# Conformer convolution stage: VectorE's taps kept out of the norms, the residual's bias and the rounding moved, two taps fewer for GpSimd

## The chip, the cores and the metric

One core of one Trainium2 chip runs the whole program. The metric is the device time of one execution in microseconds (us), as the median of three runs. TensorE (PE in the rows) multiplies, VectorE (DVE), ScalarE (ACT) and GpSimd (POOL) do the elementwise work, and SyncE's queue (SP) issues the DMAs.

## What is computed

Two layers of a diffusion trunk over 1024 latent tokens of width 1024, with 256 context tokens. Layer 0 mixes with differential attention and Fourier groups, layer 1 with a Conformer convolution; each is followed by a SwiGLU feed-forward. The change touches layer 1's mixer and the beginning of its feed-forward:

```python
def conformer_conv(h, pw1_w, pw1_b, dw_w, dw_b, ln_g, ln_b, pw2_w, pw2_b):
    a, g = jnp.split(h @ pw1_w + pw1_b, 2, axis=-1)
    u = a * jax.nn.sigmoid(g)
    u = depthwise_conv(u, dw_w) + dw_b          # 31 taps along the tokens, per channel
    u = jax.nn.silu(layernorm(u, ln_g, ln_b))
    return u @ pw2_w + pw2_b

x = x + mod_l[2] * conformer_conv(modulate(rmsnorm(x, mix_norm_g), mod_l[0], mod_l[1]), ...)
x = x + mod_l[5] * swiglu(modulate(rmsnorm(x, ffn_norm_g), mod_l[3], mod_l[4]), w1, w3, w2)
```

## The kernel before

Activations lie transposed: a tile is 128 channels by 512 tokens, so a tensor is 8 channel tiles (j = 0 to 7) in two halves of the tokens (h = 0, 1). Every product is made exact enough by splitting both operands into a rounded part and a rest (`hh`, `hl` for activations, `wh`, `wl` for weights, `uh`, `ul` for the feed-forward's hidden tiles): three matmuls of 512 columns for one (L95 to L97). The rounded part is a copy that rounds, the rest a subtraction. TensorE's order is written by hand from the end of layer 0 on. On the other engines a scheduler places what is not marked with `keep`; what is marked stays in the order in which it was written.

The convolution stage runs in this order on TensorE.

- **Cells**: the products of pw1, one per channel tile and half. ScalarE takes the sigmoid (`sig`, L1269), VectorE the gated product `u` (L1271), and then the 31 taps of the tile are shared out. GpSimd takes `NPA` = 11 taps of half 0 and `NPB` = 12 of half 1: ScalarE scales a window (`pr`, L1191), GpSimd adds it to `acc` (L1192). VectorE takes the others as chains in PSUM (`cs`, L1158, L1161), then joins GpSimd's sum (L1167) and writes the tile (`acc`, L1170). A planner with rough costs (`work`, `took`, `clock`) decides, each time that TensorE gets a block of work, how many taps VectorE and GpSimd get behind it.
- **Layer norm of half 0**: `ln_first` subtracts the mean on VectorE (L1296), squares on ScalarE (L1298) and sums on TensorE (L1299). `neg_rstd` makes the reciprocal root, `ln_apply` multiplies (L1328), takes Silu (L1329), rounds to `hh` (L1331) and subtracts to `hl` (L1332). Two cells stand between sum and use.
- **pw2 of half 0** (`pw2_half`): eight products; the first two together, channel tile by channel tile, as `hh` and `hl` arrive. The residual `xt` has gate times bias added (L1351), each product is flushed into it (L914), squares are summed on VectorE (`nacc`), and one matmul (L180) sums them over the channels for the next norm. One cell, then `norm_apply` (L1377 to L1388).
- **Units**: the feed-forward of half 0 begins while taps of half 1 still run. A unit f makes one hidden tile (48 matmuls, then `gate`: L940 to L943), a unit j adds two output tiles (24 matmuls, flushed by L914). They come as four f, four j, and so on. `while left(1): unit(...)` goes on until no tap of half 1 is left; then come mean, `ln_center`, `ln_var`, `ln_apply` and pw2 of half 1, with `POSB` units between them, and the last units.

The lists `LNH` and `LNL` say, channel tile by channel tile, whether VectorE makes `hh` and `hl` in `ln_apply`, or ScalarE and GpSimd.

## Time and profile before

| | |
|---|---|
| time, median of 3 runs (lowest to highest) | 2589.54 us (2587.44 to 2596.87) |
| the profiled execution: time, span | 2593.21 us, 2591.4 us |
| TensorE busy, share of the span | 2494.8 us, 96% |
| VectorE, ScalarE, GpSimd | 1428.6 us (55%), 1039.0 us (40%), 1025.1 us (40%) |
| granted TensorE clock, mean | 0.984 |

The span is the profiled time from the first to the last instruction; 1.8 us of the execution lie around it. Matmuls are pipelined, so that TensorE's busy time does not say that it runs at its peak; the count of matmuls in a stretch, set against their spacing, tells more. The clock is given as a share of 2.4 GHz; its two levels are 2.4 and 1.2 GHz.

### The profile page before, as it was taken

How to read it: one execution, taken by the hardware profiler on the slowest of the kernel's cores; microseconds unless marked ns; L12 is line 12 of the kernel's file. 1: busy time of each engine (PE TensorE's matmuls, PEld its weight loads, DVE VectorE, ACT ScalarE, POOL GpSimd, SP SyncE). 2: the span in 40 equal slices, each digit the busy share in tenths (PEclk: the TensorE clock that was granted, in tenths of full speed). 3: DMA queues.
4: the chain of work that ended last, by engine and by line, in shares of the span. 5: the costliest groups of instructions: out<-in, count | busy, mean ns of one | idle time of the engine just before them, and what ended most of it. 6: DMA issues, size and time to landing. Idle time of an engine off the chain costs nothing.

```text
span 2591.4 us, 30933 instructions
## 1 busy us (share of the span) xinstructions
PE 2494.8 (96%) x11818; PEld 2036.1 (79%) x11818; DVE 1428.6 (55%) x2028; ACT 1039.0 (40%) x1808; POOL 1025.1 (40%) x682
## 2 busy tenths in 40 slices
PE   8999979999999999999999999888998999999998
PEld 4788968778788888888788779666776788888887
DVE  4777359999564327262733569877946522222225
ACT  6321158988452121212121477565545422221113
POOL 2534032333443223232322358376982344431223
PEclk9999999999999999999999999989999999999999
DMA  9556643331522325242432355412333333321113
GB/s 342 190 181 223 185 140 81 83 90 31 165 66 90 114 78 175 82 146 81 149 96 71 115 169 181 139 58 81 98 90 106 94 94 97 98 81 49 46 47 120
DMA packets 350989, 299.35 MB, mean 116 GB/s; under 512 B 12341, under 2 KB 318458, under 8 KB 350842
## 3 DMA queue, kind: packets, MB, share of 16 engines
q1 hardware_dynamic: 349658, 293.16, 37.0%
q0 software_dynamic: 1184, 4.23, 0.5%
q8 instruction: 93, 1.52, 0.2%
q14 instruction: 54, 0.44, 0.1%
HBM read 259.07 MB, written 38.27 MB: 115 GB/s over the span
## 4 chain that ended last, share of the span: by engine, by line
PE 71%; DVE 7%; ACT 3%; POOL 2%; DMA 2%; issue 1%; DVEq 0%; SPq 0%; ACTq 0%; POOLq 0%
PE ps L97 20%; PE ps L95 20%; PE ps L96 20%; PE o L768 3%; PE s L740 2%; PE pst L751 2%; DVE p L886 1%; POOL acc L1192 1%; DVE cs L1161 1%; DVE acc L159 1%; PE sx L740 1%; POOL p L874 1%; DMA aw<-in_ada_w_dram 1%; ACT wh L85 1%; PE ps L809 0%
## 5 line engine op out<-in xcount | busy, mean ns | idle before, releaser
L86 POOL TENSOR_TENSOR wl<-wr,wh 128x1024 fp32r<-128x1024 f32 (+1 forms) x225 | 528.2, 2348 | 983.1 <-ACT wh L85 910.4
L95 PE MATMUL ps<-hh,wh 128*128 128x512 f32 (+2 forms) x2200 | 858.7, 390 | 15.6 <-ACT hh L1331 8.9
L97 PE MATMUL ps<-hl,wh 128*128 128x512 f32 (+2 forms) x2200 | 851.6, 387 | 9.3 <-POOL hl L1332 2.8
L96 PE MATMUL ps<-hh,wl 128*128 128x512 f32 (+2 forms) x2200 | 848.0, 386 | 3.2 <-DMA wl<-pd 2.0
L95 PEld LDWEIGHTS ps<-hh,wh 128*128 128x128 f32 x2200 | 416.5, 189 | 106.5 <-ACT hh L1331 10.9
L97 PEld LDWEIGHTS ps<-hl,wh 128*128 128x128 f32 x2200 | 416.6, 189 | 103.5 <-POOL hl L1332 5.4
L85 ACT CAST wh<-wr 128x1024 fp32r<-128x1024 f32 (+1 forms) x238 | 243.2, 1023 | 627.1 <-PE ps L97 467.6
L96 PEld LDWEIGHTS ps<-hh,wl 128*128 128x128 f32 x2200 | 417.3, 190 | 92.5 <-issue 3.1
L941 DVE TENSOR_TENSOR us<-us,ps 128x512 f32<-128x512 f32 x88 | 60.5, 687 | 596.5 <-PE ps L97 589.6
L95 PE MATMUL ps<-uh,wh 128*128 128x512 f32 (+1 forms) x728 | 281.8, 388 | 3.8 <-ACT uh L942 2.1
L97 PE MATMUL ps<-ul,wh 128*128 128x512 f32 (+1 forms) x728 | 279.8, 385 | 3.9 <-DVE ul L943 3.9
L96 PE MATMUL ps<-uh,wl 128*128 128x512 f32 (+1 forms) x728 | 278.1, 383 | 0.0
L1192 POOL TENSOR_TENSOR acc<-acc,pr 128x512 f32<-128x512 f32 x168 | 226.1, 1349 | 27.9 <-ACT pr L1191 19.7
L963 DVE SCALAR_TENSOR_TENSOR xt<-ps,mod,xt 128x512 f32<-128x512 f32 (+1 forms) x176 | 125.6, 722 | 131.4 <-PE ps L97 131.2
L159 DVE SCALAR_TENSOR_TENSOR acc<-aw,sc,acc 128x256 f32<-128x256 f32 x280 | 186.0, 664 | 20.0 <-DMA aw<-in_ada_w_dram 12.7
L1161 DVE SCALAR_TENSOR_TENSOR cs<-u,dwc,cs 128x512 f32<-128x512 f32 x280 | 194.8, 748 | 2.0 <-POOL u L1414 0.3
L943 DVE TENSOR_TENSOR ul<-us,uh 128x512 fp32r<-128x512 f32 x88 | 152.5, 1732 | 62.3 <-ACT uh L942 62.3
L97 PEld LDWEIGHTS ps<-ul,wh 128*128 128x128 f32 x728 | 137.1, 188 | 33.4 <-DVE ul L943 5.2
L95 PEld LDWEIGHTS ps<-uh,wh 128*128 128x128 f32 x728 | 137.1, 188 | 32.2 <-ACT uh L942 2.9
L96 PEld LDWEIGHTS ps<-uh,wl 128*128 128x128 f32 x728 | 137.2, 189 | 28.1 <-issue 0.7
L940 ACT ACTIVATE us<-ps 128x512 f32<-128x512 f32 x88 | 52.6, 598 | 252.9 <-PE ps L97 252.8
L874 POOL TENSOR_SCALAR p<-p,r 128x1280 f32<-128x1280 f32 x48 | 63.9, 1332 | 172.1 <-DVE r L873 132.2
(292 smaller groups left out, 3080.4 us busy)
## 6 DMA issues: line engine op xcount, KB each, us to landing
wr<-in_w_dram SPq DMA_DIRECT2D x162, 512.0 KB, 3.8
aw<-in_ada_w_dram SPq DMA_DIRECT2D x96, 512.0 KB, 4.2
wr<-in_pw_dram SPq DMA_DIRECT2D x64, 512.0 KB, 4.3
wl<-pd SPq DMA_DIRECT2D x32, 512.0 KB, 3.6
q<-qd SPq DMA_DIRECT2D x96, 128.0 KB, 2.9
wr<-in_w_dram SPq DMA_DIRECT2D x28, 384.0 KB, 3.2
wr<-in_w_in_dram SPq DMA_DIRECT2D x20, 512.0 KB, 4.3
wr<-in_w_out_dram SPq DMA_DIRECT2D x16, 512.0 KB, 4.2
```

The costliest lines, as they stand in the source:

```text
L85: S.copy(hi, src)
L86: (lo_eng or G).tensor_tensor(lo, src, hi.bitcast(F32), op=ALU.subtract)
L95: PE.matmul(ps, wh, xh, start=first, stop=False)
L96: PE.matmul(ps, wl, xh, start=False, stop=False)
L97: PE.matmul(ps, wh, xl, start=False, stop=last)
L159: V.scalar_tensor_tensor(a, aw[:, k, :], s1, a, op0=ALU.mult, op1=ALU.add)
L740: keep(PE.matmul(o, q[qt // 4][v][:, c, (qt % 4) * P:(qt % 4 + 1) * P], kk[:, c, k0:k0 + n], start=(v == 0), stop=(v == 1)))
L874: keep(G.tensor_scalar(y["p"][0], y["p"][0], r[:, 0:1], 1.0, op0=ALU.mult, op1=ALU.mult))
L943: V.tensor_tensor(ul, s, uh.bitcast(F32), op=ALU.subtract)
L963: V.scalar_tensor_tensor(XT[j][h][:, c], ps, mcol(self.l, 5, j), XT[j][h][:, c], op0=ALU.mult, op1=ALU.add)
L1161: keep(V.scalar_tensor_tensor(c["ps"], win(j, h, i), tap(i, j), c["ps"], op0=ALU.mult, op1=ALU.add))
L1192: keep(G.tensor_tensor(csum(j, h), csum(j, h), pr, op=ALU.add))
```

## The change

It has five parts. A list `quiet` stops the planner from handing taps to VectorE: from the end of half 0's taps until its pw2 begins, and again from pw2's seventh product until `norm_apply` is done. The gated bias `gb` is computed early, and the eight bias additions to the residual of half 0, not marked with `keep` and so free to go as early as `gb` exists, stand among the cells. ScalarE makes all eight `hh` of a layer norm, VectorE the `hl` of even tiles, GpSimd of odd ones, and ScalarE's steps keep their written order. GpSimd takes 10 taps of a half 1 tile and VectorE 21. The last square of a residual is no longer added on VectorE: TensorE sums `nacc` and that square in two matmuls. In units j the two outputs alternate by hidden tile. `POSB` becomes (0, 1, 2).

```diff
-NPA, NPB = 11, 12
+NPA, NPB = 11, 10
...
-LNH = (0, 1)
-LNL = (1, 1, 0, 1, 0, 1, 0, 1)
+LNL = (1, 0, 1, 0, 1, 0, 1, 0)
 NEG, NEF = 3, 3
-POSB = (0, 2, 1)
+POSB = (0, 1, 2)
...
-            d = chain() if clock["dve"] < t - TDVE / 2 else None
+            d = chain() if clock["dve"] < t - TDVE / 2 and not quiet else None
...
             keep(V.tensor_tensor(t, t, y, op=ALU.mult))
-            S.activation(t, t, AF.Silu, bias=vc1[:, LNB + j:LNB + j + 1], scale=vc1[:, LNG + j:LNG + j + 1])
+            keep(S.activation(t, t, AF.Silu, bias=vc1[:, LNB + j:LNB + j + 1], scale=vc1[:, LNG + j:LNG + j + 1]))
             hi, lo = VH[j]
-            (V.tensor_copy if LNH[j % 2] else S.copy)(hi, t)
+            keep(S.copy(hi, t))
             (V if LNL[j] else G).tensor_tensor(lo, t, hi.bitcast(F32), op=ALU.subtract)
...
-        add(KT - 1)
-        return acc
+        return [acc, nsq[KT - 1]]
...
     while len(cells) > 2 * NDEF:
+        if len(cells) == 22:
+            keep(V.tensor_tensor(gb, mod[:, 1, 16:24], vc1[:, PW2B:PW2B + 8], op=ALU.mult))
         step()
...
     finish(0)
+
+    quiet.append(1)
     cells_until(clock["dve"])
...
     VH = ln_apply(0, y)
-    keep(V.tensor_tensor(gb, mod[:, 1, 16:24], vc1[:, PW2B:PW2B + 8], op=ALU.mult))
     took(12.0, 2.0)
     second.append(1)
     while len(cells) > HOLD:
         step(keep)
+    quiet.clear()
...
-            for i in range(2):
-                for k in range(GROUPS[g]):
+            for k in range(GROUPS[g]):
+                for i in range(2):
...
-                if between and i == 0:
+                if between and k == 0:
                     between()
...
-    acc = pw2_half(0, VH, w2, None, lambda j: (work(11.0 if j == 0 else 0 if j == 1 else 5.5, 0.2 if j < 6 else -4.0), took(1.4 + (1.5 if j < 5 else 0))))
+    def rstd_of(parts):
+        ps = smps()
+        for i, t in enumerate(parts):
+            PE.matmul(ps, ones, t, start=(i == 0), stop=(i == len(parts) - 1))
+        return neg_rstd(None, HF, 1.0 / D, nw, ps)
+
+    acc = pw2_half(0, VH, w2, None, lambda j: (quiet.append(1) if j == 6 else None, work(11.0 if j == 0 else 0 if j == 1 else 5.5, 0.2), took(1.4 + (1.5 if j < 5 else 0))))
     while len(cells) > HOLD - HOLB:
         step()
-    y = neg_rstd(acc, HF, 1.0 / D, nw, smps())
+    y = rstd_of(acc)
     while cells:
         step()
     unit_weights(V)
     F.HH[0] = norm_apply(0, y)
+    quiet.clear()
...
-    unit(between=lambda: y.append(neg_rstd(acc, HF, 1.0 / D, nw, smps())))
+    unit(between=lambda: y.append(rstd_of(acc)))
```

How the instructions stand, at three places. The line numbers of the changed kernel are lower by one or two here. First VectorE at the layer norm of half 0, before: the two `cs` chains belong to half 1, the eight subtractions of the mean (`acc<-acc,pq`) follow, then the two steps of the reciprocal root, and taps again.

```order
L1161 SCALAR_TENSOR_TENSOR cs<-u_12490,dwc,cs 128x512
L1161 SCALAR_TENSOR_TENSOR cs<-u_12497,dwc,cs 128x512
L1161 SCALAR_TENSOR_TENSOR cs<-u_12490,dwc,cs 128x512
L1296 TENSOR_TENSOR acc<-acc,pq 128x512 x8
L185 SCALAR_TENSOR_TENSOR ny_14189<-ps,ny_14189 128x512
L187 SCALAR_TENSOR_TENSOR ps<-ny_14189,ny_14187 128x512
L1161 SCALAR_TENSOR_TENSOR cs<-u_12497,dwc,cs 128x512
L1161 SCALAR_TENSOR_TENSOR cs<-u_12490,dwc,cs 128x512
```

The same place now, from the last tile of half 0 (`acc<-u_13756`) on.

```order
L1169 SCALAR_TENSOR_TENSOR acc<-u_13756,dwc,cs 128x512
L1157 TENSOR_SCALAR cs<-u_12490,dwc,vc_78 128x512
L1157 TENSOR_SCALAR cs<-u_12497,dwc,vc_78 128x512
L1160 SCALAR_TENSOR_TENSOR cs<-u_12490,dwc,cs 128x512
L1160 SCALAR_TENSOR_TENSOR cs<-u_12497,dwc,cs 128x512
L1295 TENSOR_TENSOR acc<-acc,pq 128x512 x6
L1160 SCALAR_TENSOR_TENSOR cs<-u_12490,dwc,cs 128x512
L1295 TENSOR_TENSOR acc<-acc,pq 128x512 x2
L1160 SCALAR_TENSOR_TENSOR cs<-u_12497,dwc,cs 128x512
L184 SCALAR_TENSOR_TENSOR ny_14183<-ps,ny_14183 128x512
L186 SCALAR_TENSOR_TENSOR ps<-ny_14183,ny_14181 128x512
L1270 SCALAR_TENSOR_TENSOR u_13613<-ps,vc_78,sig 128x496
```

Thirteen operations of half 1 stood between the last tile and the first subtraction; now four do, and two more stand among and behind the subtractions. Of the ten taps between the root and the first multiplication none is left, only `u`.

Second, ScalarE in `ln_apply` of half 0, before: `wh` is a rounded weight tile for pw2, L1329 is Silu, L1331 its rounding.

```order
L85 CAST wh<-wr 128x1024
L1329 ACT_TABLE_LOAD
L1329 ACTIVATE acc<-acc,vc_78 128x512
L1331 CAST hh_14268<-acc 128x512
L1329 ACTIVATE acc<-acc,vc_78 128x512
L1191 ACTIVATE pr<-u_12490,dwc 128x512 x3
L1329 ACTIVATE acc<-acc,vc_78 128x512 x2
```

And now:

```order
L1328 ACT_TABLE_LOAD
L1328 ACTIVATE acc<-acc,vc_78 128x512
L1330 CAST hh_14252<-acc 128x512
L84 CAST wh<-wr 128x1024
L1328 ACTIVATE acc<-acc,vc_78 128x512
L1330 CAST hh_14254<-acc 128x512
L1328 ACTIVATE acc<-acc,vc_78 128x512
L1330 CAST hh_14256<-acc 128x512
L1190 ACTIVATE pr<-u_12490,dwc 128x512
```

The weight tile's rounding moved behind the first tile's, and each Silu has its own rounding right behind it.

Third, VectorE at the RMS norm between pw2 of half 0 and the first unit, before: the root's second step, then the ends and beginnings of four tap chains, then `na`, the first operand of the norm's use.

```order
L187 SCALAR_TENSOR_TENSOR pq<-ny_14715,ny_14713 128x512
L1170 SCALAR_TENSOR_TENSOR acc<-u_12490,dwc,cs 128x512
L1170 SCALAR_TENSOR_TENSOR acc<-u_12497,dwc,cs 128x512
L1158 TENSOR_SCALAR cs<-u_12695,dwc,vc_78 128x512
L1158 TENSOR_SCALAR cs<-u_12886,dwc,vc_78 128x512
L1161 SCALAR_TENSOR_TENSOR cs<-u_12695,dwc,cs 128x512
L1161 SCALAR_TENSOR_TENSOR cs<-u_12886,dwc,cs 128x512
L1377 SCALAR_TENSOR_TENSOR na<-xt_6884,gm,pq 128x512
```

And now, from the flush of the last product (`xt_6898`) on:

```order
L913 SCALAR_TENSOR_TENSOR xt_6898<-ps,mod,xt_6898 128x512
L85 TENSOR_TENSOR wl<-wr,wh 128x1024
L184 SCALAR_TENSOR_TENSOR ny_14702<-pq,ny_14702 128x512
L186 SCALAR_TENSOR_TENSOR pq<-ny_14702,ny_14700 128x512
L1375 SCALAR_TENSOR_TENSOR na<-xt_6884,gm,pq 128x512
L1375 SCALAR_TENSOR_TENSOR na<-xt_6886,gm,pq 128x512
L1375 SCALAR_TENSOR_TENSOR na<-xt_6888,gm,pq 128x512
L1270 SCALAR_TENSOR_TENSOR u_13757<-ps,vc_78,sig 128x496
L1386 SCALAR_TENSOR_TENSOR hl_14768<-na,mod,hh_14767 128x512
```

The six operations of half 1's taps are gone from between the root and its use; the last cell's `u` stands ahead of the first `hl` in both. Further on, the mean of half 1 stands behind the tenth unit f, where it stood behind the eleventh; VectorE has 176 tap operations for half 1 where it had 160, and at the first unit's gate 161 of them are still to come, where 110 were.

## Rows read from the trace of the kernel before

**Rows 1.** Stretches: length, busy time of PE, PEld, DVE, ACT, POOL, clock, DMA, GB/s.

```profile
1540.00:1667.20 127.20, 127.20 (x769) 112.34 (x767) 114.14 (x170) 81.41 (x122) 85.83 (x74) 1.00 0.57 174
1667.20:1719.80 52.60, 37.28 (x113) 23.77 (x113) 35.59 (x49) 29.70 (x42) 27.46 (x18) 0.81 0.10 31
1719.80:1754.80 35.00, 33.74 (x145) 26.74 (x143) 29.14 (x33) 26.15 (x39) 27.25 (x18) 1.00 0.35 105
1754.80:1787.00 32.20, 22.66 (x76) 16.50 (x77) 25.52 (x36) 18.74 (x26) 13.38 (x9) 0.84 0.17 49
1787.00:1945.00 158.00, 155.37 (x673) 125.56 (x672) 106.42 (x145) 74.50 (x102) 148.38 (x88) 1.00 0.32 95
1945.00:1970.70 25.70, 22.30 (x82) 16.14 (x81) 17.96 (x20) 10.98 (x16) 7.66 (x4) 0.93 0.31 96
1970.70:1998.60 27.90, 20.57 (x73) 14.66 (x72) 15.42 (x23) 17.07 (x25) 9.49 (x5) 0.88 0.36 112
1998.60:2040.00 41.40, 39.92 (x174) 32.34 (x174) 23.25 (x25) 16.13 (x22) 4.78 (x2) 1.00 0.35 103
```

**Rows 2.** TensorE's waits from 1660 to 2000: us in total, times, longest.

```profile
PE ps L95 <- ACT hh L1331: 8.9, 4, 3.9
PE ps L1299 <- ACT nsq L1298: 7.2, 1, 7.2
PE pq L180 <- DVE nacc L1346: 4.3, 1, 4.3
```

**Rows 3.** Timeline of TensorE at the layer norm of half 0.

```profile
1674.42 8.72 PE L1299 MATMUL ps<-nsq,ones 128*128 128x512 f32 x16 [7.21 <-ACT nsq L1298]
```

**Rows 4.** Timeline of ScalarE among the cells: start, us, instruction, idle before it.

```profile
1585.92 1.05 ACT L1028 CAST wh<-wr 128x1024 fp32r<-128x1024 f32 x1 [1.22 <-PE ps L97]
```

**Rows 5.** Timeline of VectorE at the layer norm of half 0.

```profile
1665.79 7.33 DVE L1161 SCALAR_TENSOR_TENSOR cs<-u,dwc,cs 128x512 f32<-128x512 f32 x11
1673.03 4.86 DVE L1296 TENSOR_TENSOR acc<-acc,pq 128x512 f32<-128x512 f32 x8
```

**Rows 6.** Timeline of ScalarE from half 0's Silu to its bias additions.

```profile
1694.06 1.04 ACT L85 CAST wh<-wr 128x1024 fp32r<-128x1024 f32 x1 [3.21 <-PE ps L97]
...
1696.42 0.81 ACT L1329 ACTIVATE acc<-acc,vc 128x512 f32<-128x512 f32 x1
1697.27 0.62 ACT L1331 CAST hh<-acc 128x512 fp32r<-128x512 f32 x1
...
1717.41 5.02 ACT L1351 ACTIVATE xt<-xt,gb 128x512 f32<-128x512 f32 x8 [2.28 <-DVE gb L1466]
```

**Rows 7.** Timeline of VectorE: two of the subtractions that make `hl`.

```profile
1706.56 0.69 DVE L1332 TENSOR_TENSOR hl<-acc,hh 128x512 fp32r<-128x512 f32 x1
...
1710.18 1.66 DVE L1332 TENSOR_TENSOR hl<-acc,hh 128x512 fp32r<-128x512 f32 x1
```

**Rows 8.** Timeline of VectorE at the RMS norm of half 0.

```profile
1763.38 1.40 DVE L1170 SCALAR_TENSOR_TENSOR acc<-u,dwc,cs 128x512 f32<-128x512 f32 x2
...
1767.44 2.06 DVE L1377 SCALAR_TENSOR_TENSOR na<-xt,gm,pq 128x512 f32<-128x512 f32 x3
```

**Rows 9.** Timeline of ScalarE at the same norm.

```profile
1767.20 0.68 ACT L1269 ACTIVATE sig<-ps,vc 128x496 f32<-128x496 f32 x1 [3.89 <-PE ps L97]
1767.78 1.04 ACT L85 CAST wh<-wr 128x1024 fp32r<-128x1024 f32 x1
```

**Rows 10.** Timeline of VectorE between two units f.

```profile
1800.46 9.30 DVE L1161 SCALAR_TENSOR_TENSOR cs<-u,dwc,cs 128x512 f32<-128x512 f32 x14
```

**Rows 11.** VectorE's waits from 1787 to 1945, taps alone.

```profile
DVE cs L1167 <- POOL acc L1192: 5.1, 3, 2.6
```

**Rows 12.** The page's groups: busy us, mean ns of one, idle before.

```profile
L1192 POOL TENSOR_TENSOR acc<-acc,pr 128x512 f32<-128x512 f32 x168 | 226.1, 1349 | 27.9 <-ACT pr L1191 19.7
...
L943 DVE TENSOR_TENSOR ul<-us,uh 128x512 fp32r<-128x512 f32 x88 | 152.5, 1732 | 62.3 <-ACT uh L942 62.3
```

**Rows 13.** The chain that ended last, at the reload of half 1's residual.

```profile
1980.75 3.44 DMA xt<-xd
```

More of the change, by code (lines that the diff above doesn't have):

```diff
@@ L1140, in trunk_kernel @@
     dq, pq = [[], []], [[], []]
-    active, latest, pool_on, second = [], [None], [], []
+    active, latest, pool_on, second, quiet = [], [None], [], [], []
     drained, pooled, done0 = set(), {}, []
```

## The prediction

> **What bounds the kernel.** The page comes first (the table above): TensorE is busy for 96% of the span, VectorE for 55%, ScalarE and GpSimd for 40%. An engine beside TensorE can cost time only where TensorE waits for it, so the second view is the table of stretches around the norms of layer 1 [rows 1]: length, the five engines' busy time (TensorE, its weight loads, VectorE, ScalarE, GpSimd), granted clock. In the cells (first row) TensorE is busy throughout. In the units (fifth row) it is busy for 155.4 of 158.0 us, and 155.4 us over 673 matmuls give their pitch, 0.231 us. From it the others are measured: 48 matmuls (a unit f, two cells, or a pair of pw2's products) are 11.1 us, 24 (a unit j, one cell or product) 5.5.
>
> The second stretch, 52.6 us, holds the sum of the layer norm (8.7 us for 16 records in [rows 3], some 7 at full clock by the stretch's 0.81), two cells and a pair: 29 us of work, so 23.5 are lost. The fourth, 32.2 us, holds a sum of two records, a cell and a unit f: 17.5, so 14.7 lost. The sixth and seventh, 53.6 us, have 155 records, eight of them at about half a microsecond like those of [rows 3]: 38, so some 16 lost. Part of each loss is clock: 0.81, 0.84, 0.93 and 0.88 of 2.4 GHz, while it is 1.00 in the busy stretches. After 2040 nothing comparable stands. So there are about 54 us to be had, and the list of TensorE's waits [rows 2] names whom it waits for: ScalarE's `hh` (8.9), the layer norm's squares (7.2), `nacc` (4.3). For each I then read the timeline of the engine that is late.
>
> **The change, part by part.**
>
> *Biases among the cells.* The eight additions take 5.02 us on ScalarE [rows 6]. The order now puts them ahead of a rounding of weights that ran at 1585.92 for 1.05 us behind an idle 1.22 [rows 4]. They could delay it by 5.02 − 1.22 = 3.8 us, and a cell's weights with it; if the weights have that much lead the cost is nothing. I take 1.4, toward the lower end, since TensorE had no wait there [rows 1] and one tile's delay is made up only once. **−1.4 (−3.8 to 0).**
>
> *Layer norm of half 0.* The mean's sum is ready at 1667.2, where TensorE stops, but VectorE is in eleven taps of 7.33 us and begins to subtract at 1673.03 [rows 5]; TensorE waits 7.2 for the squares and starts at 1674.42 [rows 3], 1.4 behind the first subtraction. Now four taps stand between half 0's last tile and the subtractions, and they run before the mean is ready; with one more tap amid them the sum goes from 1668.7 to 1676.9 (8.2 even at the slow pace). The root's four steps take about 2.7 us, an estimate from operations of that size (0.62 to 0.68 [rows 6, 9]). The first of two cells ends at 1682.4; its `sig` and the weight rounding (0.68 and 1.04 [rows 9]), a scaled window and a table load go before Silu in ScalarE's order, which puts the first Silu at 1686.1. Before it stood at 1696.42, behind a weight rounding at 1694.06 that had waited 3.2 for TensorE [rows 6]: 10.3 earlier. From there the old chain took 21.0 us to the bias additions at 1717.41. The new one on ScalarE is eight times Silu and `hh` (0.81 + 0.62), nine windows at 0.63 (the spacing of the bias additions), and a weight tile: 18.2, and some 3 of waits for GpSimd's alternating additions and `hl` (1.35 each [rows 12]), 21 again. So the pair ends at about 1709.5, not 1719.8. The additions at 1717.41 also delayed the next weight tiles: the third stretch has 1.3 us without TensorE [rows 1], which goes. **+11.6 (6.5 to 15).** The low end is a chain 5 us longer, four waits of 1.35 on GpSimd; the high end one without the 3 us of waits.
>
> Here a rule speaks against the change, which now gives VectorE four and GpSimd four `hl`, with GpSimd's additions between. A row first: two of VectorE's `hl` took 0.69 and 1.66 us [rows 7], the same operation on the same shape. The Trainium skill ("SBUF — State Buffer", section "Who interferes with whom") says that a VectorE instruction with two inputs in SBUF and a GpSimd instruction that reads SBUF exclude each other, the later one waiting for the whole of the other, while one with a single SBUF input is not touched. The row agrees. By the rule each of the four could pay the 0.97 between the two, and this term would be 11.6 − 3.9 = 7.7 if nothing hid it; I keep 11.6, because VectorE's `hl` need not be the late one of a pair.
>
> *RMS norm of half 0.* TensorE waits 4.3 for `nacc` [rows 2]; then six tap operations run from 1763.38 until `na` at 1767.44 [rows 8], 4.1 us; `sig` and the weight rounding come at 1767.20 behind an idle 3.89 [rows 9], and `hh` behind both. Now the last square goes straight to TensorE, which adds a second fp32 matmul (two records, 0.9), and no tap stands between. The sum ends 2.7 behind pw2 (square 0.6, wait for the flush 0.6, two matmuls), the cell 5.5 later, `sig`, weight rounding and the first `hh` 2.4 later still; the unit's 48 matmuls then need 11.1, plus some 2.5 while `hh` and `hl` arrive at less than TensorE's pace. That is 24.2 in place of 32.2, say 24.7. **+7.5 (5 to 12).** The low end is the wait and the taps at half their worth, the high end nearly all of the 14.7.
>
> *Units.* VectorE has 161 tap operations to do here where it had 110. The pitch of a tap is 9.30 / 14 = 0.664 [rows 10] while GpSimd is busy for 148.4 of 158.0 us [rows 1]. Until the tenth f ends there are nine f and eight j, 9 × 11.1 + 8 × 5.5 = 144 us. VectorE's load: 161 × 0.664 = 106.9, 16 flushes at the same pitch 10.6, nine gates at 0.66 + 1.73 (`ul`, [rows 12]) = 21.5, together 139. It fits by 5 us and hardly more. GpSimd has 16 additions of 1.35 less, 21.6 of its 148.4, so VectorE's 5.1 us of waits for it [rows 11] go; they were not TensorE's. TensorE loses 2.6 here [rows 1], where a j follows f at once and waits for the last `ul`. Outputs that alternate by hidden tile give that `ul` two products' time more, which removes most of it. **+1.9 (−9 to +2.6);** the lower end is `ul` at twice its shorter measure, below.
>
> *Layer norm and pw2 of half 1.* The loss is 16. The mean is asked for behind the tenth f instead of the eleventh, and with `quiet` or no taps left VectorE goes to the centring at once. I leave 0.7 for the mean, 0.7 for the variance, 4.6 for the pair (the bias additions of half 1 wait on ScalarE for the residual's reload of 3.44 us [rows 13], ahead of `hh`), and half a microsecond of slow clock. **+9.5 (6 to 13),** between a pair that waits 8 and one that waits 1.5.
>
> *The rest.* The RMS norm of half 1 gains a wait for `nacc` and pays 0.9 for a matmul: **+0.4 (−0.9 to 1.5).** New short waits leave stretches below full clock, which I put at **−1 (−3 to 0).**
>
> **Sum.** −1.4 + 11.6 + 7.5 + 1.9 + 9.5 + 0.4 − 1 = 28.5. The profiled execution took 2593.2 us, with 1.8 around its span of 2591.4; it becomes 2564.7. It lies 3.7 above the median, so against that 2589.5 − 28.5 = **2561 us**.
>
> **Rivals.** *VectorE becomes the bound in the units.* If `ul` costs 2.4 us beside GpSimd (two inputs in SBUF, as the `hl` of 1.66 against 0.69 [rows 7], on top of 1.73), nine gates take 27.5 and the load 145 is already over 144; with flushes half as slow again, 5 more, and the waits of a starting chain it is some 9 us over. The mean then comes 9 late, TensorE stands, and 2561 becomes about 2571. Against it: taps and flushes have one input in PSUM and kept their pitch beside a busy GpSimd.
>
> *The norms get no shorter.* ScalarE's chain with GpSimd's `hl` paces the pair at its old end, and only the 7.2, half the RMS norm's and half of half 1's loss go: 7.2 + 3.7 + 4.7 − 1 = 14.6, so 2575. For it: the chain from Silu to its end has the same 21 us by my own count, so it rests on Silu coming earlier.
>
> *Slower.* VectorE's taps themselves slow down. At a pitch of 0.79 with `ul` at 2.4 the load is 127.2 + 10.6 + 27.5 = 165, 21 over; the lost 28.5 need a pitch of 0.84 (28.5 over 144), from which the time is 2590 or more. At 0.92 it is 13 us over that, about 2602. Against it stands the 0.664 of [rows 10]. That the taps do not leave the norms can be excluded: the order has six left where 23 stood.
>
> **Chances and range.** Forecast, a gain of 16 to 40: 0.80. VectorE as the bound: 0.10. Norms no shorter: 0.07. Slower: 0.03. Half a per cent, 12.9 us, is about what a measurement of this kernel can tell from no change, that is below 2576.6. Nearly all of the first two cases, and a part of the third, lie below it: faster 0.88, same 0.09, slower 0.03. The terms' bounds do not all fall the same way; the largest, 5 below on the layer norm, 11 on the units and 3.5 on half 1, taken as independent, are 13 together, and upward 3.4, 4.5 and 3.5 make 7. With rival one inside, and most of rival two, the range is 2548 to 2577.
>
> **What would show it.** The first subtraction of half 0 at about 1667, TensorE's wait for squares under 2 us; no idle of several microseconds ahead of ScalarE's first Silu; the first pair of pw2 done 42 us after the mean's sum and not 52.6; the unit f done 25 us behind pw2 and not 32.2; VectorE almost without idle until the tenth f, then a mean for which TensorE waits under 2 us; no wait over 5 us at half 1's pair. I am wrong if the mean comes late by more than 5 us, if `ul` of VectorE grows beyond 2 us, or if GpSimd's `hl` ends the pair.

## The result and the profile after

The changed kernel takes 2565.67 us (median of four runs, 2564.60 to 2566.67) where the kernel before, in as many, takes 2590.76: a ratio of 0.9899, 95% interval 0.9887 to 0.9911. The profiled execution took 2565.46 us, and its span is 2563.7 us, 27.7 less than that of the profiled execution before. The forecast of 2561 us lay 5 us low, within its range.

The stretches of the changed kernel, cut at the same events as [rows 1] (length, busy time of the five engines, granted clock, DMA share, GB/s):

```profile
1540.00:1666.80 126.80, 126.77 (x767) 111.97 (x765) 114.75 (x170) 85.51 (x129) 85.45 (x74) 1.00 0.57 175
1666.80:1707.90 41.10, 33.32 (x113) 22.53 (x114) 18.69 (x27) 29.85 (x42) 24.14 (x17) 0.92 0.13 39
1707.90:1741.10 33.20, 33.20 (x144) 26.62 (x142) 27.89 (x26) 22.46 (x33) 31.87 (x20) 1.00 0.37 111
1741.10:1774.40 33.30, 23.55 (x77) 16.38 (x77) 20.10 (x21) 20.32 (x30) 16.34 (x11) 0.79 0.17 48
1774.40:1918.50 144.10, 144.10 (x626) 117.07 (x624) 133.73 (x195) 60.60 (x80) 120.46 (x69) 1.00 0.32 96
1918.50:1965.50 47.00, 42.79 (x174) 31.88 (x173) 29.85 (x37) 32.30 (x46) 19.87 (x11) 1.00 0.40 126
```

Stretch by stretch against [rows 1]: the cells are as they were (the small difference was there before them). The layer norm of half 0 to the end of pw2's first pair went from 52.6 to 41.1 us, the rest of pw2 from 35.0 to 33.2 without any idle. The fourth stretch, from pw2's end to the end of the first unit f, did not get shorter at all: 32.2 before, 33.3 now, at a clock of 0.79. The units took 158.0 with ten f and now take 144.1 with nine, so 2.8 us less for equal work (an f is 11.1), and TensorE has no idle in them. In half 1 the way from the mean's request to the beginning of the RMS norm's sum took 90.7 us for 300 matmuls (69.3 us at 0.231) and the four fp32 ones, and takes 82.0 for 318 (73.5): what it loses beside its matmuls fell from some 21 to 8.5 us, 12.8 less. These are 13.3, −1.1, 2.8 and 12.8 us, together the change of the span to within 0.1.

TensorE's waits of the changed kernel from 1660 to 2010 (us in total, times, longest), which answer to [rows 2]:

```profile
PE ps L96 <- POOL hl L1331: 5.2, 4, 3.2
PE pq L1522 <- DVE nacc L1345: 4.2, 1, 4.2
PE ps L94 <- ACT hh L1330: 3.8, 3, 1.5
...
PE pq L1522 <- ACT nsq L1364: 2.1, 1, 2.1
PE ps L1298 <- ACT nsq L1297: 1.4, 1, 1.4
```

The wait for the layer norm's squares fell from 7.2 to 1.4 us, that for `hh` from 8.9 to 3.8. The wait for `nacc` is still 4.2, and the last square, which now goes to TensorE by itself, adds a wait of 2.1 behind it. In the layer norms, GpSimd's `hl` has taken the first place: in half 0 the longest wait, 3.2, and the pair's last one, 0.6, are for it.

The two matmuls of the RMS norm's sum, in TensorE's timeline:

```profile
1745.30 1.86 PE L1522 MATMUL pq<-nacc,ones 128*128 128x512 f32 x2 [4.18 <-DVE nacc L1345]
1749.26 2.08 PE L1522 MATMUL pq<-nsq,ones 128*128 128x512 f32 x2 [2.10 <-ACT nsq L1364]
```

pw2 ends at 1741.1 and the sum 10.2 us behind it; in the kernel before it ended 5.8 us behind. What stands behind the sum is shorter than before, by some 3 us up to the unit's end, and that is used up.

The three rows of VectorE's timeline at the end of pw2 in the changed kernel show why `nacc` is late:

```profile
1741.50 2.08 DVE L85 TENSOR_TENSOR wl<-wr,wh 128x1024 fp32r<-128x1024 f32 x1 [2.22 <-ACT wh L84]
1743.50 1.75 DVE L1345 TENSOR_TENSOR nacc<-nacc,nsq 128x512 f32<-128x512 f32 x1
1745.17 0.74 DVE L913 SCALAR_TENSOR_TENSOR xt<-ps,mod,xt 128x512 f32<-128x512 f32 x1
```

pw2's last product is done at 1741.1, but its flush (the third row) stands behind a weight subtraction that waited for ScalarE, and behind a sum of squares. Both read two tiles in SBUF. ScalarE's timeline at the same place:

```profile
1739.81 0.73 ACT L1190 ACTIVATE pr<-u,dwc 128x512 f32<-128x512 f32 x1 [0.97 <-POOL acc L1191]
1740.43 1.03 ACT L84 CAST wh<-wr 128x1024 fp32r<-128x1024 f32 x1
...
1744.73 0.72 ACT L1190 ACTIVATE pr<-u,dwc 128x512 f32<-128x512 f32 x1 [1.48 <-POOL acc L1191]
1746.40 0.72 ACT L1190 ACTIVATE pr<-u,dwc 128x512 f32<-128x512 f32 x1 [0.95 <-POOL acc L1191]
1747.03 1.03 ACT L84 CAST wh<-wr 128x1024 fp32r<-128x1024 f32 x1
1747.97 0.72 ACT L1190 ACTIVATE pr<-u,dwc 128x512 f32<-128x512 f32 x1
1748.59 0.61 ACT L1364 ACTIVATE nsq<-xt 128x512 f32<-128x512 f32 x1
```

ScalarE makes windows (`pr`) for GpSimd's taps of half 1 and waits for GpSimd to free their buffers, 1.48 and 0.95 us here; the weight rounding and the last square queue behind them. GpSimd's own timeline from pw2's last products on, in the changed kernel:

```profile
1736.78 15.84 POOL L1191 TENSOR_TENSOR acc<-acc,pr 128x512 f32<-128x512 f32 x10
1759.02 2.37 POOL L85 TENSOR_TENSOR wl<-wr,wh 128x1024 fp32r<-128x1024 f32 x1 [6.40 <-ACT wh L84]
```

And at the same norm in the kernel before, GpSimd's timeline, at which the prediction had not looked:

```profile
1744.50 8.39 POOL L1192 TENSOR_TENSOR acc<-acc,pr 128x512 f32<-128x512 f32 x5
1764.86 1.31 POOL L1177 TENSOR_TENSOR sm<-acc 128x512 f32<-128x512 f32 x1 [11.97 <-DVE acc L1170]
```

One of VectorE's sums of squares there:

```profile
1758.31 0.68 DVE L1346 TENSOR_TENSOR nacc<-nacc,nsq 128x512 f32<-128x512 f32 x1
```

Before, GpSimd stood still for 12 us through this norm, because its next instruction, the sum `sm` over half 1's first tiles, waited for the end of VectorE's chains [rows 8], and the sum of squares took 0.68 us. Now those chains end later and `sm` stands further on, and ten additions run through the norm's beginning.

### The profile page after: what moved, and what is told of

Its sections match the earlier page's. It is cut to its first block, busy times and chain, and to the rows that moved or that the text cites. A ratio compares the mean times of both kernels' runs of the same rounds, so it can differ in the third digit from the quotient of the medians.

```text
span 2563.7 us, 30908 instructions
## 1 busy us (share of the span) xinstructions
PE 2487.0 (97%) x11822; PEld 2035.0 (79%) x11822; DVE 1434.6 (56%) x2032; ACT 1032.3 (40%) x1800; POOL 1005.9 (39%) x668
## 4 chain that ended last, share of the span: by engine, by line
PE 81%; DVE 6%; ACT 3%; POOL 3%; DMA 2%; issue 1%; SPq 0%; DVEq 0%; POOLq 0%; ACTq 0%
PE ps L96 23%; PE ps L94 23%; PE ps L95 23%; PE o L767 3%; PE s L739 3%; PE pst L750 2%; POOL acc L1191 2%; DVE acc L158 1%; DVE p L885 1%; PE sx L739 1%; DMA aw<-in_ada_w_dram 1%; POOL p L873 1%; DMA q<-qd 1%; DVE mm L857 1%; PE ps L808 0%
## 5 line engine op out<-in xcount | busy, mean ns | idle before, releaser
L1191 POOL TENSOR_TENSOR acc<-acc,pr 128x512 f32<-128x512 f32 x152 | 206.5, 1362 | 22.8 <-ACT pr L1190 14.9
L1160 DVE SCALAR_TENSOR_TENSOR cs<-u,dwc,cs 128x512 f32<-128x512 f32 x296 | 204.4, 747 | 1.9 <-POOL u L1412 0.3
L939 ACT ACTIVATE us<-ps 128x512 f32<-128x512 f32 x88 | 52.6, 598 | 252.7 <-PE ps L96 252.6
```

Of the source, the lines that this page charges most:

```text
L1160: keep(V.scalar_tensor_tensor(c["ps"], win(j, h, i), tap(i, j), c["ps"], op0=ALU.mult, op1=ALU.add))
L1191: keep(G.tensor_tensor(csum(j, h), csum(j, h), pr, op=ALU.add))
```

## The experiments

All were timed in rounds against the kernel before, whose median in the three groups of runs was 2591.3, 2591.9 and 2591.5 us. Theory 1 is that the RMS norm of half 0 is held up by GpSimd's taps; theory 2 that its own new form makes it late (flush, last square, a second matmul). Where an edit is undone, the rest is the changed kernel. The length of the way ahead of the mean's sum differs from one profiled execution to the next by up to 9 us (the sum ends between 1662.6 and 1671.9), so stretches are compared beside the times. The profiled execution of e4_no_quiet_ln lies 4.5 us below its median, those of c5_both_npb9, e7_bias_late and e8_j_order 5 to 6 above theirs, so that there the stretches need not add up to the difference of the medians. The loss of half 1 is reckoned as above: the length from the mean's request to the beginning of the RMS norm's sum, less 0.231 us for each matmul that is not fp32.

**GpSimd kept out of the RMS norm** (c1_calm).

```diff
-            p = pool_next() if clock["pool"] < t else None
+            p = pool_next() if clock["pool"] < t and not calm else None
...
-            S.activation(pr, win(j, h, i0 + i), AF.Copy, scale=tap(i0 + i, j))
+            (keep if h else lambda i: i)(S.activation(pr, win(j, h, i0 + i), AF.Copy, scale=tap(i0 + i, j)))
...
-(quiet.append(1) if j == 6 else None, work(
+((quiet.append(1), calm.append(1)) if j == 6 else None, work(
```

`calm` ends with `quiet`, and half 0's squares (L1364) are kept in order too.

> From pw2's seventh product until the RMS norm of half 0 is done, GpSimd gets no taps either, and ScalarE's windows of half 1 and its squares keep their written order. Theory 1 (GpSimd's additions run on through this norm; ScalarE's windows wait for them ahead of weight roundings and of the last square, and VectorE's weight subtractions and sums of squares are stretched by them): the stretch from pw2's end to the end of the first unit f falls from 33.3 us to 25 to 28, the sum ends 3 to 4 us behind pw2 and not 10.2, and the time falls by 5 to 8, to 2558 to 2561, unless the 14 or so displaced additions make GpSimd late at the tenth unit f (then up to 5 us of it come back there). Theory 2 (the sum is late by its own form, the flush, the last square and the second matmul): the stretch stays at 32 to 34, the time at 2564 to 2568.

Measured: 2557.69 us, ratio 0.9870 (0.9855 to 0.9884). The two stretches from pw2's end, and VectorE's timeline there:

```profile
1738.40:1765.10 26.70, 21.93 (x78) 16.19 (x77) 15.71 (x19) 14.80 (x20) 5.36 (x3) 0.87 0.15 43
1765.10:1909.40 144.30, 143.99 (x624) 116.70 (x622) 135.13 (x195) 71.47 (x96) 137.19 (x82) 1.00 0.32 96
```

```profile
1735.50 0.68 DVE L1345 TENSOR_TENSOR nacc<-nacc,nsq 128x512 f32<-128x512 f32 x1
1738.62 0.75 DVE L913 SCALAR_TENSOR_TENSOR xt<-ps,mod,xt 128x512 f32<-128x512 f32 x1 [2.44 <-PE ps L96]
1739.70 1.23 DVE L85 TENSOR_TENSOR wl<-wr,wh 128x1024 fp32r<-128x1024 f32 x1 [0.32 <-ACT wh L84]
```

And TensorE's timeline:

```profile
1738.42 1.02 PE L1522 MATMUL pq<-nacc,ones 128*128 128x512 f32 x2
1740.25 1.13 PE L1522 MATMUL pq<-nsq,ones 128*128 128x512 f32 x2 [0.81 <-ACT nsq L1364]
```

The stretch is 26.7 us instead of 33.3, the sum ends 3 us behind pw2, `nacc` takes 0.68 instead of 1.75 and is done before the last product, the flush follows the product at once, and `wl` takes 1.23 instead of 2.08. GpSimd does the displaced additions in the units, 137 of 144 us, and TensorE loses next to nothing by it. Theory 1 holds and theory 2 falls: the same form of sum is not late without GpSimd's additions and the windows that ScalarE makes for them. The two edits that keep an order are not what did it: the program built with `calm` alone has, from pw2's sixth square to the norm's end, the same order on ScalarE, and throughout the same on VectorE and TensorE (it was not timed). How the gain divides between GpSimd's additions and ScalarE's windows is not shown, since `calm` takes both away.

**More buffers for the windows** (c2_npr).

```diff
-NPR = 3
+NPR = 6
```

> GpSimd's scaled windows have six buffers in place of three, so that ScalarE waits less for GpSimd, while GpSimd's additions run on. Theory 1a (ScalarE's queue is what delays the norm): the last square comes 2 to 4 us earlier, and the stretch from pw2's end to the first unit f's end falls from 33.3 to 29 to 31, time 2562 to 2564. Theory 1b (it is VectorE's instructions with two inputs that GpSimd's additions stretch): sums of squares stay at 1.75 us, weight subtractions at 2.0, the stretch at 32 to 34. Theory 2: unchanged too.

Measured: 2568.44 us (0.9909, 0.9894 to 0.9924). The waits for `nacc` and the last square are 2.8 and 2.8 us in place of 4.2 and 2.1; from pw2's end to the first `hh` it is 18.1 us, 18.5 in the changed kernel. `nacc` takes 1.77 us and `wl` 2.07. So room in the ring of windows alone gives nothing: ScalarE still waits 1.48 and 0.96 us for GpSimd ahead of the same weight rounding and the last square, and the stretched VectorE instructions stay, as theory 1b had it.

**The ban lifted for the RMS norm** (e3_no_quiet_rms): the `quiet.append(1)` at `j == 6` is left out.

> The ban on VectorE's taps is lifted for the RMS norm of half 0 and kept for the layer norm. The prediction's term of 7.5 us for this norm would have been lost (2573). Theory 1: the ban gained nothing here, because GpSimd and ScalarE set the end; taps that come back cost at most the 4 us that six of them take between root and use: the stretch is 33 to 37 us and the time 2565 to 2569, with the units unchanged. Theory 2: the same taps cost 3 to 4 us, 2569.

Measured: 2565.82 us (0.9900, 0.9883 to 0.9916), and the waits for `nacc` and the last square are 4.4 and 1.9. In time the ban here is worth nothing, but not for the reason expected. The wait for the first `hh` and `hl` grows from 2.3 and 1.2 to 2.8 and 2.5, and from pw2's end to the end of the unit f it is 2.4 us longer. The units, which were to stay as they were, hold 576 matmuls instead of 624: VectorE's taps are done sooner, the mean of half 1 is asked for one unit f earlier, 342 matmuls instead of 318 cover half 1's way, and its loss falls from 8.5 to 4.7 us. So the ban shortens this norm and lengthens the other. Whether it would gain something with GpSimd held as in c1_calm, no run shows.

**The ban lifted for the layer norm** (e4_no_quiet_ln): the first `quiet.append(1)` is left out.

> The ban is lifted for the layer norm of half 0 and kept for the RMS norm: 11 taps again stand ahead of the subtractions of the mean, ten between the root and the first multiplication. By the prediction's term the stretch from the mean's sum to the end of the pair rises from 41.1 by 5 to 7 us (the taps' 7.3 less what runs before the mean is ready, and what the cells hide), the time to 2571 to 2573. Rival (ScalarE's rounding and its order alone made this gain): the stretch stays within 2 us of 41, time 2565 to 2568.

Measured: 2577.48 us (0.9945, 0.9929 to 0.9960). VectorE's timeline:

```profile
1664.57 7.33 DVE L1160 SCALAR_TENSOR_TENSOR cs<-u,dwc,cs 128x512 f32<-128x512 f32 x11
1671.81 4.86 DVE L1295 TENSOR_TENSOR acc<-acc,pq 128x512 f32<-128x512 f32 x8
```

These are the rows of before [rows 5] again, TensorE waits 7.2 us for the squares again, and from the mean's sum to pw2's end it is 88.7 us instead of 74.4. The size was more than expected: of the 14.4 us, 7.5 are there when VectorE comes to the root (`ny`), 4.3 more at the first Silu and the rest in the chain behind it. Some 6 us of the 14.4 come back further on: from pw2's end to the end of the span it is 816.4 us, 822.5 in the changed kernel. About 3.5 come from the RMS norm of half 0 and as much from half 1, which loses 5.0 instead of 8.5, since here too its mean is asked for one unit f earlier; 1 goes off elsewhere.

**The last square on VectorE again** (e2_one_matmul).

```diff
-        return [acc, nsq[KT - 1]]
+        add(KT - 1)
+        return [acc]
```

> The last square of a residual is added on VectorE again, and one matmul sums. Theory 1: the addition takes 1.7 us beside GpSimd where the second matmul took some 0.9 to 2, so the first hh of half 0's norm moves by -0.5 to +1.5 us and half 1's by -0.5 to +1; time 2564.5 to 2568. Theory 2 (the two matmuls made the sum late): the stretch from pw2's end to the first hh falls from 18.5 us by 2 or more, time 2561 to 2564.

Measured: 2571.04 us (0.9917, 0.9901 to 0.9933, which reaches into the interval of the changed kernel); by the median both expectations missed. From pw2's end to the first `hh` it is 21.8 us instead of 18.5. TensorE waits 10.7 us for `nacc` in half 0 and 2.8 in half 1. VectorE's timeline:

```profile
1749.16 2.04 DVE L85 TENSOR_TENSOR wl<-wr,wh 128x1024 fp32r<-128x1024 f32 x1 [2.19 <-ACT wh L84]
1751.13 1.74 DVE L1345 TENSOR_TENSOR nacc<-nacc,nsq 128x512 f32<-128x512 f32 x1
```

I had counted the addition's own time. The addition also stands behind the last weight subtraction in VectorE's order, and that waits for a rounding on ScalarE.

**12 taps for GpSimd again** (e5_npb12): `NPA, NPB = 11, 12`.

> GpSimd takes 12 taps of a half 1 tile again, VectorE 19. By the prediction's term for the units: GpSimd gets 21.6 us more of additions and fills its 120 of 143 us, VectorE loses 10.6 of its 134; half 1's mean is asked for at the tenth unit f or later, waits 1 to 4 us for GpSimd's sum, and the time rises by 1 to 5 us, to 2567 to 2571. Rival (GpSimd has run so far ahead during the RMS norm that the two additions more fit, and the ban and the order made the gain): 2564 to 2567. With theory 1 the RMS norm itself can only become longer, since GpSimd has more to add there.

Measured: 2576.27 us (0.9941, 0.9925 to 0.9957), more than any theory had said. TensorE's waits from 1760 to 2014:

```profile
PE ps L94 <- ACT hh L1330: 5.3, 2, 2.8
PE ps L96 <- DVE ul L942: 2.5, 2, 1.7
PE pq L1320 <- DVE lsq L1314: 1.7, 1, 1.7
```

2.5 us are waits for `ul` in the units, as the kernel before had them. The rest is half 1: the mean is asked for a unit f later, and so the three units that are left to fill the norm are one f and two j instead of two f and one j, 5.5 us less of cover. From the mean's request to the RMS norm's sum TensorE takes 84.8 us for 24 matmuls fewer than in the changed kernel's 82.0, which is 8 us more lost for equal work.

**The layer norm's rounding as before** (e6_rounding): `LNH` and `LNL` and the two lines of Silu and `hh` are those of before.

> The layer norm's rounding goes back: VectorE makes hh of odd tiles and five hl, GpSimd three, and ScalarE's steps are no longer held in the written order. By the prediction (the first Silu comes earlier because of the ban, and ScalarE's chain then takes as long as the old one) the stretch from the mean's sum to pw2's end stays within 3 us of 74.4, time 2564 to 2569. Rival (the rounding on ScalarE makes a good part of the gain in the norms): the stretch grows by 3 to 7 us, and half 1's by 2 to 4, time 2570 to 2576.

Measured: 2565.00 us (0.9898, 0.9882 to 0.9915); from the mean's sum to pw2's end 74.1 us instead of 74.4. In half 0 the rounding moved nothing. In half 1 this execution loses 12.1 us, 8.5 in the changed kernel and 8.5 to 10.6 in the runs that leave half 1's code and the number of its matmuls alone; that is what the rival had said for half 1, but the time does not show it, and so it stays open there.

**The bias behind the norm's products again** (e7_bias_late): `gb` is computed behind `ln_apply(0, y)` as before.

> The gated bias and the eight additions to half 0's residual go back behind the layer norm's products, the rest as in the changed kernel. By the prediction's terms: 1.4 us less in the cells (-3.8 to 0; the trace after shows no wait there, so 0 is likelier), 1 to 2 us more behind the first pair of pw2, where ScalarE spends 5.0 us on them ahead of weight roundings, time 2564 to 2569. Rival (the additions now cover nothing and cost nothing in either place): within 1 us of 2565.7.

Measured: 2571.04 us (0.9927, 0.9915 to 0.9940); both expectations missed. ScalarE's timeline:

```profile
1703.90 0.81 ACT L1328 ACTIVATE acc<-acc,vc 128x512 f32<-128x512 f32 x1 [0.43 <-DVE acc L1327]
1704.62 4.99 ACT L1350 ACTIVATE xt<-xt,gb 128x512 f32<-128x512 f32 x8
1709.51 0.71 ACT L1190 ACTIVATE pr<-u,dwc 128x512 f32<-128x512 f32 x1
1710.12 0.60 ACT L1330 CAST hh<-acc 128x512 fp32r<-128x512 f32 x1
```

The eight additions, free to go as soon as `gb` exists, now land between the last Silu and its `hh`, and TensorE waits 6.3 us there; from the mean's sum to pw2's end it is 82.8 us instead of 74.4. Before they came behind the chain [rows 6].

**Outputs of units j one behind the other** (e8_j_order): the two loops as before.

> In units j the two outputs stand one behind the other again, the rest as in the changed kernel. By the prediction (TensorE lost 2.6 us in the units, waiting for the last ul, and alternating outputs remove most of it) the units get 2 to 4 us longer, with waits for ul of 0.5 to 1.7 us at two to four places, time 2567 to 2570. Rival (VectorE is ahead now, and ul comes in time in either order): within 1 us of 2565.7.

Measured: 2568.62 us (0.9919, 0.9906 to 0.9931), an interval that overlaps that of the changed kernel. The units take 3.9 us more, and the trace has the waits expected, which the changed kernel has not:

```profile
PE ps L96 <- DVE ul L942: 2.8, 3, 1.7
...
PE ps L94 <- ACT uh L941: 1.7, 2, 1.3
```

**GpSimd kept out of both norms.** Three tries on top of c1_calm. c3_hl_first writes pw2's first three weight tiles ahead of `ln_apply`, so that the additions follow the last `hl` on GpSimd:

```diff
+    w2 = [prep(col(I["pw2"], j * P))() for j in range(3)]
     VH = ln_apply(0, y)
...
-            (V if LNL[j] else G).tensor_tensor(lo, t, hi.bitcast(F32), op=ALU.subtract)
+            (lambda i: i if LNL[j] else keep(i))((V if LNL[j] else G).tensor_tensor(lo, t, hi.bitcast(F32), op=ALU.subtract))
...
-    w2 = [prep(col(I["pw2"], j * P))() for j in range(3)]
```

> The kernel of c1_calm, in which moreover GpSimd makes its four hl of half 0's layer norm before it begins half 1's additions (the weight tiles of pw2 are rounded ahead of the layer norm's products, and the order of GpSimd is written out). Theory 1, extended (GpSimd's additions among the hl are what draws out the layer norm's chain too: VectorE's hl of 1.4 to 1.8 us beside them, a wait of 3.3 us for GpSimd's first hl, ScalarE's windows between Silu and rounding): from the mean's sum to pw2's end 73.7 us fall by 4 to 7, VectorE's hl cost 0.7 us each, and the time falls from c1_calm's 2557.7 by 3 to 6, to 2552 to 2555, if the seven displaced additions (9.5 us) don't make GpSimd late at half 1's mean; if they do, up to 4 us come back there. Rival (ScalarE's own chain of eight Silu and eight roundings sets the pair's end): 0 to 2 us less, 2556 to 2558.

Measured: 2564.75 us (0.9894, 0.9879 to 0.9908), 7 slower than c1_calm, so that both expectations missed. VectorE's `hl` did fall to 0.69 us each; the second of the four, in c1_calm and in c3_hl_first:

```profile
1688.01 1.46 DVE L1331 TENSOR_TENSOR hl<-acc,hh 128x512 fp32r<-128x512 f32 x1 [2.32 <-ACT hh L1330]
...
1691.51 0.69 DVE L1331 TENSOR_TENSOR hl<-acc,hh 128x512 fp32r<-128x512 f32 x1 [2.30 <-ACT hh L1330]
```

But the third weight rounding stood ahead of the first Silu and waited for TensorE:

```profile
1683.47 1.04 ACT L84 CAST wh<-wr 128x1024 fp32r<-128x1024 f32 x1 [3.21 <-PE ps L96]
1684.53 1.28 ACT L1328 ACT_TABLE_LOAD   x1
1685.83 0.81 ACT L1328 ACTIVATE acc<-acc,vc 128x512 f32<-128x512 f32 x1
```

And the late additions ran into the RMS norm again, where the wait for `nacc` is back at 4.2 us. c4_both_calm mends both (two weight tiles ahead, the third kept behind the `hl`; `took(12.0, 14.0)` for `took(12.0, 2.0)`), and c5_both_npb9 gives GpSimd nine taps besides.

> The kernel of c1_calm with GpSimd's four hl of half 0's layer norm ahead of half 1's additions, as in c3_hl_first, but with the third weight tile left behind the first rounding (in c3_hl_first it stood ahead of the first Silu and cost some 4 us) and with the planner told that GpSimd starts 12 us later (there its additions ran on into the RMS norm again, with a wait of 4.2 us). Theory 1: both norms free of GpSimd's additions; from the mean's sum to pw2's end 69 to 71 us (c1_calm 73.7), from there to the first hh 10.5 to 11.5 (c1_calm 10.7), time 2552 to 2556, since the mean of half 1 comes two units later and these units are work that has to be done anyway. Rival (GpSimd's lost 10 to 15 us come back in the units and at half 1's mean, whatever is written): 2558 to 2564.

> The kernel of c4_both_calm with 9 taps of a half 1 tile for GpSimd and 22 for VectorE: 10.8 us less on GpSimd, 5.3 more on VectorE. By theory 1 the norms are as in c4_both_calm; if GpSimd sets when half 1's taps end, the mean comes one unit earlier and the time is 0 to 3 us lower than there; if VectorE does (135 of 144 us in c1_calm's units), ul of the units come late and it is 1 to 5 higher.

Measured: 2571.08 us (0.9925, 0.9912 to 0.9939) and 2561.30 us (0.9889, 0.9875 to 0.9902); no time expected for either of the two held. Both norms of half 0 are nearly as expected: 71.4 us from the mean's sum to pw2's end in either (c1_calm 73.7), 10.7 from there to the first `hh`. But in c4_both_calm the mean of half 1 comes two units later, and the unit between mean and variance is then a j of 24 matmuls and not an f of 48. TensorE's waits there:

```profile
PE pq L1320 <- DVE lsq L1314: 8.4, 1, 8.4
```

With nine taps it is an f again, that wait is 1.7 us, and the time falls by 10. It is still not better than c1_calm, whose mean comes one unit earlier yet. So c4_both_calm lost more than even its rival had said, and in another way: what is missing is the cover of units in half 1's norm, not GpSimd's time. Half 1 loses 24.1 us with 270 matmuls on its way (c4_both_calm), 16.2 and 16.9 with 294 (c5_both_npb9, e5_npb12), 8.5 to 12.1 with 318, and 4.7 and 5.0 with 342 (e3_no_quiet_rms, e4_no_quiet_ln): 24 matmuls more go with 4 to 8 us less, so the place of the mean is worth as much as a norm's whole repair.

## Why the prediction was right, and where it was not

The sum was 28.5 us and the spans differ by 27.7. That this is so near is luck: one term was 8.6 us too high, and the others, each 1 to 3 us too low, make up 7.9 of it. Most of the 5 us by which the forecast missed the median comes from elsewhere. Against the profiled executions it is 0.8 off (2564.7 forecast, 2565.5 measured); but it went on to the median of before, 3.7 us lower, while the profiled execution of the changed kernel lies at its own median.

*Biases among the cells*, −1.4: measured nothing. The additions do stand ahead of the weight rounding, which runs at 1589.44 instead of 1585.92, 3.5 us later; but TensorE has no idle in the stretch, so the cell's weights had that lead.

*Layer norm of half 0*, +11.6: 11.5 in the norm and 1.8 behind it. The first subtraction stands at 1666.8 (predicted 1667), the first Silu at 1684.4 (1686.1), the pair ends 41.1 us behind the mean (42):

```profile
1666.81 3.67 DVE L1295 TENSOR_TENSOR acc<-acc,pq 128x512 f32<-128x512 f32 x6
...
1684.37 0.81 ACT L1328 ACTIVATE acc<-acc,vc 128x512 f32<-128x512 f32 x1
```

e4_no_quiet_ln shows that the ban is the cause, e6_rounding that the rounding is not. What I did not see is that the new chain needs the early bias: with `gb` late the additions fall into it, and the way to pw2's end is 8.4 us longer (e7_bias_late). One of the signs of being wrong that the prediction names did appear, GpSimd's `hl` as the pair's last wait; that wait was 0.6 us, and the pair still ended where it was forecast.

*RMS norm of half 0*, +7.5 (5 to 12): measured −1.1. This is the step that failed, in the words "The sum ends 2.7 behind pw2 (square 0.6, wait for the flush 0.6, two matmuls)": it ends 10.2 behind, and the unit f 33.3 behind pw2 instead of 25. I had gone through VectorE's order at this place and taken GpSimd and ScalarE as they were before, when GpSimd happened to wait for `sm`. The line in which the diff drops the planner's early stop at the last two products (`0.2 if j < 6 else -4.0`) is not the cause: in the program built with it written back, the instructions of TensorE, ScalarE, GpSimd and VectorE have the same order as without. c1_calm shows the term's size when GpSimd is held as well: 32.2 to 26.7, +5.5, its low end. The second matmul by itself is worth 4.4 us of waits in this norm (10.7 against 4.2 and 2.1) and 2.8 in half 1's, from which its own 0.9 goes off each time; for half 1 I had written 0.4.

*Units*, +1.9: 2.8. VectorE is busy for 133.7 of 144.1 us (139 predicted), the taps keep their pitch beside a busy GpSimd, `ul` fell from 1.6 to 1.3 us on average in this stretch. The rival in which VectorE becomes the bound did not come. Its 2.4 us for `ul` beside GpSimd, on which the −9 rests too, follows from no row; the longest of the nine took 2.0. e8_j_order shows where the waits for `ul` and `uh` went.

*Half 1*, +9.5 with 0.4: 12.8. The mean waits 0.3, the variance 1.1, the pair 2.8, instead of 0.7, 0.7 and 4.6. That it rests on the taps' number was not seen: e5_npb12 loses 8 of its 10.6 us here, because the place of the mean in the row of units decides whether an f or a j covers the norm. The second matmul gives the 2.8 less 0.9 named above; what `POSB` gives, no run shows.

*Slow clock*, −1: none in half 1 (a granted clock of 1.00, before 0.93 and 0.88), and 0.92 instead of 0.81 in the layer norm; only the RMS norm fell, from 0.84 to 0.79, with 6 us of waits for its sum. Its share lies within the stretches above.

One slip changes nothing above: the range's lower end of 2548 does not follow from the terms, which reach 7 us beyond 2561, to 2554.

The rule that I had weighed (the Trainium skill, "SBUF — State Buffer", section "Who interferes with whom") bore on a second place, to which I had not applied it. In the layer norm three of VectorE's four `hl` take 1.4 to 1.8 us in c1_calm and 0.69 in c3_hl_first, as the rule has it. With GpSimd's additions behind the `hl`, the way to pw2's end is 2.3 us shorter (c4_both_calm against c1_calm); GpSimd's own `hl` come earlier by it too, and which of the two counts is not shown. In the RMS norm `nacc` and `wl` take 1.75 and 2.08 us beside GpSimd, 0.68 and 1.23 without, and there nothing hides them.

The price of each part undone alone, by the medians: 11.8 us for the ban in the layer norm, 10.6 for the ten taps, 5.4 each for the second matmul and the early bias, 2.9 for the order of units j, nothing for the rounding and for the ban in the RMS norm. The intervals for the second matmul and the order of units j reach into that of the changed kernel, so these two are known by their waits rather than by their times. The prices add up to 36, more than the 25 of the whole, which fits that some are worth their price only beside others; no run undoes two at once.

Left open: how much of c1_calm's gain is GpSimd's additions and how much ScalarE's windows, what `POSB` gives, and whether another row of units would let c5_both_npb9's shorter norms show in the time.

## What to carry to other kernels

When an engine is told to keep out of a critical stretch, look at what the other engines do there: an engine that used to wait for the banned work may now run on through the stretch, draw out the instructions of others and fill their queues there. In an engine's order an instruction costs its own time and the wait of everything written ahead of it, so that an addition of 0.7 us could be worth 5. Filler work should be judged by the pieces of it that are left where a wait has to be covered, not by its sum.

## What was not expected of the hardware

A sum of two SBUF tiles on VectorE that met GpSimd's additions took 1.75 us instead of 0.68, and so did all six of the changed kernel's pw2 of half 0 (1.75 to 1.79); a weight subtraction took 2.08 instead of 1.23, so the two in a row ahead of a flush cost 1.9 us more. GpSimd's additions were drawn out as well: ten in a row took 15.84 us, and the mean of one over the whole kernel before was 1.35 us [rows 12].

In these rows the one that starts first goes through, and the other pays. In the changed kernel `wl` begins at 1741.50, in the middle of an addition that runs from 1741.23 to 1742.50, and takes 2.08. In e3_no_quiet_rms GpSimd's additions go on just the same, but with the taps ahead of it the same weight subtraction begins 0.08 us before an addition:

```profile
1742.70 1.22 DVE L85 TENSOR_TENSOR wl<-wr,wh 128x1024 fp32r<-128x1024 f32 x1
1742.78 2.25 POOL L1191 TENSOR_TENSOR acc<-acc,pr 128x512 f32<-128x512 f32 x1
```

It takes 1.22 us, and the addition 2.25. A sum of squares of that run that begins at 1738.14, 0.03 us ahead of an addition, takes 0.69, and the addition 1.82.
